# Attention scores by pairs of heads, the low keys on half of TensorE's rows

## The chip, the core and the metric

The kernel runs on one core of a Trainium2 chip. The metric is the device time of one execution in microseconds (us). Engines are named as the profile names them: PE is TensorE's matmul and PEld its weight load, DVE is VectorE, ACT ScalarE, POOL GpSimd, SP SyncE, whose queue here issues most DMAs.

## The reference

Two layers on 256 tokens of width 2048, with a context of 256 tokens: first a Fourier layer, then an attention layer with 64 query heads of 64, 8 key heads, a sink and a gate. The change lies in the second layer:

```python
def _attend_with_sink(q, k, v, sink, mask=None):
    s = jnp.einsum('bqhgd,bkhd->bhgqk', q, k).astype(jnp.float32) * (ATTN_HEAD_DIM ** -0.5)
    if mask is not None:
        s = jnp.where(mask, s, NEG_INF)
    sk = jnp.broadcast_to(sink.astype(jnp.float32)[None, :, :, None, None], s.shape[:-1] + (1,))
    p = jax.nn.softmax(jnp.concatenate([s, sk], axis=-1), axis=-1)[..., :-1]
    return jnp.einsum('bhgqk,bkhd->bqhgd', p.astype(v.dtype), v)
```

Queries come from `h @ w_in`, turned by their positions; the result is `y = o * silu(z)` with `z` from the same product, and then `x + gate * (y @ w_out)`. The keys of a query block are its band of 256 tokens and the 256 of the context: 512 keys.

## The kernel before

Numbers are carried in two parts, a high and a low one, each in float16 (weights, queries, keys, probabilities) or in a rounded float32; `mm3` makes a product out of three matmuls (L80 high by high, L81, L82 with one low part each).

The attention layer is a loop over 64 heads `i` (key head `hk = i // 8`, pair `b = i // 2`), with other matmuls of the layer as filling between its steps. `filler` emits the next unit of a list (`units`): eight `q` units make the queries of a key head, two `z` units a block of 128 gate columns, twelve `o` and six `b` units begin the output product. A unit takes 1024 columns of split weights; a split of 2048 columns is ScalarE's L180 (high part) and VectorE's L181 (low part) from a buffer `raw` that SP's queue loads, and serves two units. Six tiles `ws` hold three such splits.

The steps of one head `i`:

- `stage_s` (L1362): for each block `tb` of 128 queries two score matmuls of 512 keys. The stationary operand `qq[hk][:, i % 8, tb, :]` has the high part of a query on rows 0 to 63 and the low part on rows 64 to 127; the moving one is `kkh`, the high keys standing twice (L1373), and then `kkl`, the low keys standing twice (L1374). VectorE adds the mask and takes the maximum (L1375, followed by the read-out of that maximum), ScalarE takes the exponential with its sum (L1378) and a small one for the sink (L1379), VectorE adds the sums and inverts them (L1380, L1381). ScalarE then writes the high half of the probabilities (L1388), VectorE the low half (L1389), and SP's queue transposes both into `ft` (L1391, four buffers). The last two heads are transposed on TensorE instead (`stage_t`).
- `stage_o` (L1401): the values of a pair, 24 matmuls L1408 on 64 columns each, the two heads of the pair in the two halves of the columns. `emit_y` gates the result (L1360), once the `z` block has had its tanh (L1347, L1348).

Per head the loop calls `stage_s(i)`, one filler, at odd `i` the values of the pair that was scored before this one, and one more filler. `q_turn` (L1255) splits the queries of the next key head and transposes them; `k_turn` splits the second half of the keys, one block in each of the heads 9, 11, 13 and 15; GpSimd turns the queries (`roped`). `finish_q` puts `q_turn` off by some slots (`defer`).

PSUM has eight banks, all from one pool (`psum`); the probabilities `p` have three pairs' worth of single buffers (`bufs=3` with two tiles a head).

The order on each engine is set by a scheduler with a timeline of its own, except where `tc.issue_after(pe_last[0])` ties an instruction behind another on its engine. Before, that held for heads 0 to 3 alone (`held`).

Of the kernel before, what the change touches and what calls it, by code (L numbers as in the profile page):

```python
# [10 lines left out]
F32 = mybir.dt.float32  # L11
# [22 lines left out]
def tile_dit(ctx: ExitStack, tc: tile.TileContext, a: dict, out: bass.AP):  # L34
# [44 lines left out]
    def mm3(o, wh, wl, xh, xl, start, stop):  # L79
        PE.matmul(o, wh, xh, start=start, stop=False)  # L80
        PE.matmul(o, wh, xl, start=False, stop=False)  # L81
        return PE.matmul(o, wl, xh, start=False, stop=stop).ins  # L82
# [997 lines left out]
    with tc.tile_pool(name="h1", reuse_waits="tile", bufs=16) as h1p:  # L1080
# [76 lines left out]
        with tc.tile_pool(name="at", reuse_waits="tile", bufs=2) as at:  # L1157
# [19 lines left out]
            def o1_step(k, os_, wh, wl):  # L1177
                while len(yh) <= min(k + 4, NB - 1) and (len(yh) < 24 or fin):
                    y_split(len(yh))
                for tb in range(2):  # L1180
                    mm3(os_[tb], yh[k][:, tb * P : (tb + 1) * P], yh[k][:, N + tb * P : N + (tb + 1) * P], wh, wl, k == 0, k == NB - 1)
            def b_step(k, wh, wl):
                if k == 0:
                    oB.extend([psum() for _ in range(2)] for _ in range(2))
# [68 lines left out]
                qq[hk] = qT  # L1253

            def q_turn(tb, t, qT):  # L1255
                qf = actp.tile([P, 8, P], F16, tag="act", name="qf")
                t3 = t.rearrange("p (h d) -> p h d", d=64)
                S.copy(qf[:, :, 0:64], t3)
                V.tensor_tensor(qf[:, :, 64:128], t3, qf[:, :, 0:64], op=ALU.subtract)
                nc.sync.dma_start_transpose(qT[:, :, tb, :], qf.rearrange("p h d -> p (h d)"))  # L1260

            def units():
                order = [("q", 0)]
# [95 lines left out]
                    y1.append(act())  # L1359
                V.scalar_tensor_tensor(y1[blk // 2][:, (blk % 2) * N : (blk % 2 + 1) * N], oos.pop(blk)[:, 0:N], dscz[:, blk : blk + 1], szs.pop(blk), op0=ALU.mult, op1=ALU.mult)  # L1360

            def stage_s(i):  # L1362
                hk, blk, hh = i // 8, i // 2, i % 2
                kkh, kkl = (kk[hk // 4][:, hk % 4 * 2 + j].rearrange("p t q -> p (t q)") for j in range(2))
# [4 lines left out]
                so = []  # L1369
                for tb in range(2):  # L1370
                    o = psum()
                    st = qq[hk][:, i % 8, tb, :]
                    PE.matmul(o, st, kkh, start=True, stop=False)  # L1373
                    pe_last[0] = PE.matmul(o, st, kkl, start=False, stop=True).ins  # L1374
                    V.tensor_tensor_reduce(o, o, mask[:, tb, :], nscl[:, hk : hk + 1], nsink[:, i : i + 1], ALU.add, ALU.min, mx[:, tb : tb + 1])  # L1375
                    so.append(o)
                for tb in range(2):
                    S.activation(pt[tb], so[tb], AF.Exp, bias=mx[:, tb : tb + 1], scale=-1.0, accum_out=sm[:, tb : tb + 1])  # L1378
                S.activation(es, mx, AF.Exp, bias=sink[:, i : i + 1])  # L1379
                V.scalar_tensor_tensor(sm, sm, 1.0 / PS, es, op0=ALU.mult, op1=ALU.add)  # L1380
                V.reciprocal(sm, sm)  # L1381
                ft = at.tile([P, 8, 2, P], F16, tag="ft", name="ft", bufs=4)
                fs = []
                for tb in range(2):
                    f = act(F16, 1024)
                    if i >= 62:
                        fs.append(f)
                    S.activation(f[:, 0:512], pt[tb], AF.Copy, scale=sm[:, tb : tb + 1])  # L1388
                    V.scalar_tensor_tensor(f[:, 512:1024], pt[tb], sm[:, tb : tb + 1], f[:, 0:512], op0=ALU.mult, op1=ALU.subtract)  # L1389
# [11 lines left out]
            def stage_o(b):  # L1401
# [3 lines left out]
                for kb in range(4):  # L1405
                    for vp, fp_ in ((0, 0), (1, 0), (0, 1)):
                        for hh in range(2):
                            PE.matmul(  # L1408
                                oo[hh * 64 : hh * 64 + 64, 0:N],
                                v01[kb][:, hk, vp * 64 : vp * 64 + 64],  # L1410
                                fts[hh][:, fp_ * 4 + kb, :, :].rearrange("p t q -> p (t q)"),
# [27 lines left out]
                if defer and defer[0][0] + 2 < j:  # L1439
                    defer.pop(0)[1]()  # L1440

            def held(i):
                return tc.issue_after(pe_last[0]) if i < 4 else nullcontext()

            pts = {}
            for i in range(66):
                if 8 <= i < 16 and i % 2:
                    k_turn(1, ((i - 9) // 2,))
                if i % 8 == 0:
                    while defer:  # L1450
                        defer.pop(0)[1]()
                if i == 62:
# [3 lines left out]
                if i < 64:  # L1456
                    with held(i):
                        pts[i] = stage_s(i)
                if i - 2 >= 62:
                    stage_t(*pts[i - 2])  # L1460
                with held(i):
                    filler()
                if i >= 3 and i % 2:
                    with held(i):
                        stage_o((i - 3) // 2)
                with held(i):
                    filler()


        with tc.tile_pool(name="fin", reuse_waits="tile", bufs=1) as fp:  # L1470
# [207 lines left out]
```

## Time and profile before

| | |
|---|---|
| median of three runs | 1719.26 us (1718.33 to 1721.31) |
| the profiled execution | 1717.57 us, of which the span of its instructions is 1715.8 |
| granted TensorE clock | 0.999 |
| PE busy in the span | 1681.5 us (98%) |
| DVE, ACT, POOL busy | 1366.1 (80%), 1109.7 (65%), 250.5 us (15%) |
| scores and values (first score to last value) | 1120 to 1580 us of the span |

A row of the timeline has the start in us from the span's beginning, the length, the engine, the line, the operation, out<-in, the shapes, and in square brackets the idle time before it and what ended it. Matmuls are pipelined: the length of one (0.38 us for 512 columns) is longer than the distance to the next (0.22), and it is the distance that counts. On VectorE and ScalarE too a row's length overlaps the next one's start a little.

### The profile page before, as it was taken

What the parts mean: (1) busy time and instruction counts of PE and PEld (TensorE: products, weight loads), DVE (VectorE), ACT (ScalarE), POOL (GpSimd) and SP (SyncE); (2) the same over time, 40 slices, a digit from 0 to 9 for tenths busy, and PEclk for the clock granted to TensorE, in tenths of its full rate; (3) what the DMA queues carried; (4) which work ended last, traced back from release to release, by engine and by line L of the source; (5) the groups of instructions that cost most, each with busy time, mean ns of one, the idle gap of its engine ahead of it and who ended that gap; (6) DMA issues with size and microseconds to landing.
All of it is one profiled execution on the core that took longest, in us unless ns stands there. A gap on an engine that the chain in (4) does not pass through costs nothing.

```text
span 1715.8 us, 27525 instructions
## 1 busy us (share of the span) xinstructions
PE 1681.5 (98%) x10137; PEld 1054.2 (61%) x10137; DVE 1366.1 (80%) x2322; ACT 1109.7 (65%) x1739; POOL 250.5 (15%) x261
## 2 busy tenths in 40 slices
PE   6999999999999999999999999999999999999997
PEld 4669999744444444444444454466567655877886
DVE  5778988899878797677888666889988888886555
ACT  5445655576658577765766476777777777786443
POOL 0001212201101011010102100032102320342010
PEclk9999999999999999999999999999999999999999
DMA  9998999889988799899999989599999999977543
GB/s 392 417 354 249 288 265 279 277 294 357 337 283 306 265 342 278 273 344 326 360 365 356 342 289 401 176 241 240 250 229 238 244 248 232 239 204 265 195 174 145
DMA packets 323367, 487.06 MB, mean 284 GB/s; under 512 B 181344, under 2 KB 247280, under 8 KB 299680
## 3 DMA queue, kind: packets, MB, share of 16 engines
q1 hardware_dynamic: 299168, 447.29, 81.3%
q0 software_dynamic: 19920, 31.06, 7.2%
q10 hardware_dynamic: 4144, 6.95, 1.2%
q8 instruction: 79, 1.29, 0.3%
q14 instruction: 56, 0.46, 0.1%
HBM read 433.85 MB, written 12.59 MB: 260 GB/s over the span
## 4 chain that ended last, share of the span: by engine, by line
PE 36%; DVE 25%; DMA 16%; issue 12%; ACT 9%; SPq 1%; POOL 1%; ACTq 0%; POOLq 0%; DVEq 0%
PE ps L80 11%; PE ps L81 11%; PE ps L82 11%; DVE w L181 7%; DMA rawz<-in_adw 6%; DVE junk L758 5%; DVE ps L1375 3%; DVE act L1389 3%; ACT w L180 2%; DMA rawz<-in_wz 2%; DMA rawz<-in_wq 2%; DMA raw<-in_awp 2%; ACT act L1388 2%; DMA rawz<-in_wkv 2%; ACT sqd L162 1%
## 5 line engine op out<-in xcount | busy, mean ns | idle before, releaser
L758 DVE CUSTOM_DVE_ANT_0 junk<-rawz,cb 128x1024 bf16<-128x1024 f32 x224 | 273.6, 1221 | 61.5 <-DMA rawz<-in_adw 51.8
L81 PE MATMUL ps<-act,w 128*128 128x512 f16 x688 | 260.8, 379 | 0.0
L82 PE MATMUL ps<-act,w 128*128 128x512 f16 x688 | 258.2, 379 | 0.0
L80 PE MATMUL ps<-act,w 128*128 128x512 f16 x688 | 258.0, 379 | 0.0
L80 PEld LDWEIGHTS <-w 128*128 128x128 f16 x1536 | 150.3, 98 | 132.4 <-issue 3.0
L81 PEld LDWEIGHTS <-w 128*128 128x128 f16 x1536 | 150.3, 98 | 129.5
L82 PEld LDWEIGHTS <-w 128*128 128x128 f16 x1536 | 150.3, 98 | 128.1 <-issue 1.7
L181 DVE SCALAR_TENSOR_TENSOR w<-raw,adab,w 128x2048 f16<-128x2048 f32 x72 | 172.4, 2394 | 23.8 <-ACT w L180 23.5
L181 DVE SCALAR_TENSOR_TENSOR w<-raw,up,w 128x2048 f16<-128x2048 f32 (+1 forms) x68 | 151.1, 2223 | 37.8 <-ACT w L180 36.7
L162 ACT ACTIVATE rawz<-rawz 128x1024 f32<-128x1024 f32 x104 | 109.2, 1050 | 107.8 <-DMA rawz<-in_wq 55.5
L180 ACT ACTIVATE w<-raw,adab 128x2048 f16<-128x2048 f32 x72 | 143.4, 1992 | 29.9 <-PE ps L81 29.8
L1388 ACT ACTIVATE act<-p,sm 128x512 f16<-128x512 f32 x128 | 85.4, 714 | 87.5 <-DVE sm L1381 43.7
L80 PE MATMUL ps<-h,w 128*128 128x256 f16 x512 | 139.7, 273 | 0.0
L82 PE MATMUL ps<-h,w 128*128 128x256 f16 x512 | 139.6, 273 | 0.0
L81 PE MATMUL ps<-h,w 128*128 128x256 f16 x512 | 139.6, 273 | 0.0
L180 ACT ACTIVATE w<-raw,up 128x2048 f16<-128x2048 f32 (+1 forms) x68 | 128.5, 1891 | 16.8 <-PE ps L81 9.6
L166 POOL PARTITION_ALL_REDUCE tot<-wq x58 | 59.7, 1028 | 496.0 <-ACT sqd L162 496.0
L1389 DVE SCALAR_TENSOR_TENSOR act<-p,sm,act 128x512 f16<-128x512 f32 x128 | 100.1, 813 | 37.4 <-ACT act L1388 37.3
L80 PE MATMUL ps<-y,w 128*128 128x512 f16 x336 | 126.7, 379 | 1.2 <-ACT y L180 1.2
L81 PE MATMUL ps<-y,w 128*128 128x512 f16 x336 | 126.8, 379 | 0.0
L82 PE MATMUL ps<-y,w 128*128 128x512 f16 x336 | 126.8, 379 | 0.0
L68 DVE TENSOR_TENSOR wl<-raw,wh 128x1024 fp32r<-128x1024 f32 x61 | 78.8, 1297 | 56.2 <-ACT wh L67 55.6
(392 smaller groups left out, 3958.7 us busy)
## 6 DMA issues: line engine op xcount, KB each, us to landing
raw<-in_wz SPq DMA_DIRECT2D x64, 1024.0 KB, 5.8
rawz<-in_adw SPq DMA_DIRECT2D x128, 512.0 KB, 7.6
raw<-in_awp SPq DMA_DIRECT2D x32, 1024.0 KB, 12.7
rawz<-in_wq SPq DMA_DIRECT2D x64, 512.0 KB, 7.0
raw<-in_wo SPq DMA_DIRECT2D x64, 512.0 KB, 8.1
raw<-in_wq SPq DMA_DIRECT2D x32, 1024.0 KB, 5.6
raw<-in_wu SPq DMA_DIRECT2D x32, 1016.0 KB, 7.0
zq<-in_wz SPq DMA_DIRECT2D x40, 512.0 KB, 9.3
```

The source lines that it names most:

```text
L68: last_sub[0] = eng.tensor_tensor(l, src, h.bitcast(F32), op=ALU.subtract).ins
L80: PE.matmul(o, wh, xh, start=start, stop=False)
L81: PE.matmul(o, wh, xl, start=False, stop=False)
L82: return PE.matmul(o, wl, xh, start=False, stop=stop).ins
L162: sq_ins[0] = S.activation(dump, src, AF.Square, scale=scale, accum_out=col).ins
L166: GP.partition_all_reduce(tot, col, P, bass_isa.ReduceOp.add)
L180: last_cast[0] = S.activation(h, src, AF.Copy, scale=up).ins
L181: last_sub[0] = V.scalar_tensor_tensor(l, src, up, h, op0=ALU.mult, op1=ALU.subtract).ins
L758: V.tensor_tensor_reduce(junk, wf, cb[:, s], 1.0, 0.0, ALU.mult, ALU.add, acc[:, i, kh, fg * 2 + f, s : s + 1])
L1375: V.tensor_tensor_reduce(o, o, mask[:, tb, :], nscl[:, hk : hk + 1], nsink[:, i : i + 1], ALU.add, ALU.min, mx[:, tb : tb + 1])
L1388: S.activation(f[:, 0:512], pt[tb], AF.Copy, scale=sm[:, tb : tb + 1])
L1389: V.scalar_tensor_tensor(f[:, 512:1024], pt[tb], sm[:, tb : tb + 1], f[:, 0:512], op0=ALU.mult, op1=ALU.subtract)
```

## The change

Two heads of a pair are scored by one function, `stage_p`, which calls what is left of `stage_s` for each. In the queries the high part now stands on rows 0 to 63 for the even head of a pair and on rows 64 to 127 for the odd one (`q_turn`, in two halves). The low keys are multiplied first and by the high queries alone, with 64 rows for each head; then come the high keys on all 128 rows. The product of low queries with low keys is no longer made. Each pair does `stage_p`, four fillers, and the values of the pair before it at the end, so that they stand ahead of the next pair's scores. Every matmul of `stage_p` and `stage_o` is tied behind the last one (`tied`, line L1367 in the changed kernel), and all steps and fillers run under `held`. In the last two rounds the values stand after two and three fillers. `p` has four buffers.

```diff
-                    mm3(os_[tb], ...)
+                    pe_last[0] = mm3(os_[tb], ...)
...
             def q_turn(tb, t, qT):
-                qf = actp.tile([P, 8, P], F16, tag="act", name="qf")
-                t3 = t.rearrange("p (h d) -> p h d", d=64)
-                S.copy(qf[:, :, 0:64], t3)
-                V.tensor_tensor(qf[:, :, 64:128], t3, qf[:, :, 0:64], op=ALU.subtract)
-                nc.sync.dma_start_transpose(qT[:, :, tb, :], qf.rearrange("p h d -> p (h d)"))
+                qf = act(F16, 1024)
+                t3 = t.rearrange("p (g x d) -> p g x d", x=2, d=64)
+                q5 = qf.rearrange("p (g x b d) -> p g x b d", g=4, x=2, b=2)
+                for x in range(2):
+                    S.copy(q5[:, :, x, x, :], t3[:, :, x, :])
+                for x in range(2):
+                    V.tensor_tensor(q5[:, :, x, 1 - x, :], t3[:, :, x, :], q5[:, :, x, x, :], op=ALU.subtract)
+                nc.sync.dma_start_transpose(qT[:, :, tb, :], qf)
...
+            def stage_p(b):
+                hk = b // 4
+                kkh, kkl = (kk[hk // 4][:, hk % 4 * 2 + j].rearrange("p t q -> p (t q)") for j in range(2))
+                so = [[psum() for _ in range(2)] for _ in range(2)]
+                for tb in range(2):
+                    for x in range(2):
+                        r = slice(x * 64, x * 64 + 64)
+                        tied(so[x][tb], qq[hk][r, b % 4 * 2 + x, tb, :], kkl[r], start=True, stop=False)
+                for x in range(2):
+                    for tb in range(2):
+                        tied(so[x][tb], qq[hk][:, b % 4 * 2 + x, tb, :], kkh, start=False, stop=True)
+                for x in range(2):
+                    pts[b * 2 + x] = stage_s(b * 2 + x, so[x])
...
-                pt = [at.tile([P, 512], F32, tag="p", name="p", bufs=3) for _ in range(2)]
+                pt = [at.tile([P, 512], F32, tag="p", name="p", bufs=4) for _ in range(2)]
...
-                    o = psum()
-                    st = qq[hk][:, i % 8, tb, :]
-                    PE.matmul(o, st, kkh, start=True, stop=False)
-                    pe_last[0] = PE.matmul(o, st, kkl, start=False, stop=True).ins
...
-            def held(i):
-                return tc.issue_after(pe_last[0]) if i < 4 else nullcontext()
+            def held(b):
+                return tc.issue_after(pe_last[0])
...
-            for i in range(66):
+            for b in range(33):
...
+                if b < 32:
+                    with held(b):
+                        stage_p(b)
+                for j in range(5):
+                    if b == 32 and 0 < j < 3:
+                        stage_t(*pts[61 + j])
+                    if b and j == {31: 2, 32: 3}.get(b, 4):
+                        with held(b):
+                            stage_o(b - 1)
+                    if j < 4:
+                        with held(b):
+                            filler()
```

The lines of `stage_s` after the scores are the same, with other numbers: L1375 is L1390 in the changed kernel, L1378 L1392, L1379 L1393, L1380 and L1381 L1394 and L1395, L1388 L1402, L1389 L1403, L1360 L1363, L1347 and L1348 L1350 and L1351.

On TensorE, at a score in the second half of the stage, stood before the end of a unit, two blocks with two matmuls each into one bank, and the next unit:

```order
L82 MATMUL ps_13802<-h1_9979,w16_13725 128x256
L1373 LDWEIGHTS qT_13051
L1373 MATMUL ps_13885<-kk1_10583,qT_13051 128x512
L1374 LDWEIGHTS qT_13051
L1374 MATMUL ps_13885<-kk1_10583,qT_13051 128x512
```

Now the last matmul of the last pair's values is followed by four into four banks (the low keys), and four more into the same banks:

```order
L1367 MATMUL ps_13688<-ft_13449,v_10703 64x256
L1367 LDWEIGHTS qT_13094
L1367 MATMUL ps_13715<-kk1_10583,qT_13094 128x512
L1367 LDWEIGHTS qT_13094
L1367 MATMUL ps_13717<-kk1_10583,qT_13094 128x512
L1367 LDWEIGHTS qT_13094
L1367 MATMUL ps_13716<-kk1_10583,qT_13094 128x512
L1367 LDWEIGHTS qT_13094
L1367 MATMUL ps_13718<-kk1_10583,qT_13094 128x512
L1367 LDWEIGHTS qT_13094
L1367 MATMUL ps_13715<-kk1_10583,qT_13094 128x512
```

The banks of both heads are thus written at the start of the pair. On VectorE one head of the steady part read before (`x2` stands for both blocks):

```order
L1389 SCALAR_TENSOR_TENSOR act<-p,sm,act 128x512 x2
L1375 ISA ps,mx<-ps,mask,nsink,nscl 128x512
L1375 ISA mx 128x1
L1375 ISA ps,mx<-ps,mask,nsink,nscl 128x512
L1375 ISA mx 128x1
L181 SCALAR_TENSOR_TENSOR w_14500<-raw,adab,w_14499 128x2048
L1380 SCALAR_TENSOR_TENSOR sm<-sm,es 128x2
L1381 RECIPROCAL sm<-sm 128x2
```

And now, from the last of a pair's four L1390 (before them stand L1390 twice, L1403 and L1390):

```order
L1390 ISA ps,mx<-ps,mask,nsink,nscl 128x512
L1390 ISA mx 128x1
L1394 SCALAR_TENSOR_TENSOR sm<-sm,es 128x2
L1395 RECIPROCAL sm<-sm 128x2
L181 SCALAR_TENSOR_TENSOR w_14477<-raw,adab,w_14476 128x2048
L1394 SCALAR_TENSOR_TENSOR sm<-sm,es 128x2
L1403 SCALAR_TENSOR_TENSOR act<-p,sm,act 128x512 x2
L1395 RECIPROCAL sm<-sm 128x2
L1363 SCALAR_TENSOR_TENSOR act<-ps,adab,th 128x256
L181 SCALAR_TENSOR_TENSOR w_14524<-raw,adab,w_14523 128x2048
L1403 SCALAR_TENSOR_TENSOR act<-p,sm,act 128x512
```

The masks of both heads come first, one of the two splits stands between the two sums, and one probability is left over to the next pair. On ScalarE, in a pair of the same kind, before (one head) and now:

```order
L1378 ACTIVATE p,sm<-ps,mx 128x512 x2
L1379 ACTIVATE es<-mx,sink 128x2
L1388 ACTIVATE act<-p,sm 128x512 x2
L180 ACTIVATE w_14499<-raw,adab 128x2048
L1378 ACTIVATE p,sm<-ps,mx 128x512 x2
```

```order
L1392 ACTIVATE p,sm<-ps,mx 128x512 x2
L1393 ACTIVATE es<-mx,sink 128x2
L1392 ACTIVATE p,sm<-ps,mx 128x512
L180 ACTIVATE w_11644<-raw,adab 128x2048
L1392 ACTIVATE p,sm<-ps,mx 128x512
L1393 ACTIVATE es<-mx,sink 128x2
L1402 ACTIVATE act<-p,sm 128x512 x2
L180 ACTIVATE w_11691<-raw,adab 128x2048
L1402 ACTIVATE act<-p,sm 128x512 x2
```

The first split of a pair stands behind the third exponential, with the fourth behind it.

More of the change, by code (lines that the diff above doesn't have):

```diff
@@ L1368, in stage_s @@
                 es = at.tile([P, 2], F32, tag="es", name="es")
-                so = []
                 for tb in range(2):
-                    o = psum()
-                    st = qq[hk][:, i % 8, tb, :]
[L1373 to L1376, printed above, removed]
+                    V.tensor_tensor_reduce(so[tb], so[tb], mask[:, tb, :], nscl[:, hk : hk + 1], nsink[:, i : i + 1], ALU.add, ALU.min, mx[:, tb : tb + 1])
                 for tb in range(2):
@@ L1407, in stage_o @@
                         for hh in range(2):
-                            PE.matmul(
+                            tied(
                                 oo[hh * 64 : hh * 64 + 64, 0:N],
```

28 lines of the change are left out of this document (9 added, 19 removed).

## The prediction

> **What bounds the kernel now.** I read first the busy time of the attention stage between its ends, then its waits, then the timelines of TensorE, VectorE and ScalarE over a few heads.
>
> ```profile
> core 0: us, PE busy (x) PEld busy (x) DVE busy (x) ACT busy (x) POOL busy (x), PEclk, DMA share, GB/s
> 1150.00:1525.00 375.00, 372.11 (x2850) 250.04 (x2847) 336.69 (x562) 285.23 (x508) 85.78 (x63) 1.00 0.99 236
> ```
>
> TensorE looks like the bound (372 of 375 us at clock 1.00), but VectorE is busy for 90% too. The waits of the same stretch (who waited for whom, us in total, times, longest) tell more:
>
> ```profile
> ACT act L1388 <- issue: 41.6, 23, 3.1
> ACT act L1388 <- DVE sm L1381: 38.1, 25, 2.8
> DVE act L1389 <- ACT act L1388: 34.3, 48, 0.9
> PE ps L1408 <- DMA ft<-act: 2.9, 4, 1.1
> DVE ps L1375 <- PE ps L1374: 0.8, 1, 0.8
> ```
>
> VectorE and ScalarE wait for each other in nearly every head, and for TensorE once, 0.8 us. So those two keep a rhythm of their own. TensorE waits only for `ft`, the transposed probabilities that come out of that rhythm. The timeline of TensorE gives both paces (start, length):
>
> ```profile
> 1152.58 0.38 PE L1373 MATMUL ps<-kk,qT 128*128 128x512 f16 x1
> 1166.20 0.38 PE L1373 MATMUL ps<-kk,qT 128*128 128x512 f16 x1
> ...
> 1304.34 0.38 PE L1373 MATMUL ps<-kk,qT 128*128 128x512 f16 x1
> 1304.56 0.38 PE L1374 MATMUL ps<-kk,qT 128*128 128x512 f16 x1
> ...
> 1307.72 0.27 PE L82 MATMUL ps<-h,w 128*128 128x256 f16 x1
> 1307.92 1.50 PE L1408 MATMUL ps<-ft,v 128*64 128x256 f16 x24
> 1309.35 0.28 PE L80 MATMUL ps<-h,w 128*128 128x256 f16 x1
> ...
> 1390.80 0.30 PE L1408 MATMUL ps<-ft,v 128*64 128x256 f16 x1
> 1391.69 1.47 PE L1408 MATMUL ps<-ft,v 128*64 128x256 f16 x23 [0.59 <-DMA ft<-act]
> ...
> 1485.34 0.38 PE L1373 MATMUL ps<-kk,qT 128*128 128x512 f16 x1
> ```
>
> The first and the last row are heads 5 and 53: 332.8 us for 48 heads, 55.5 us for a key head (8 heads, 4 pairs). A pair without a wait took 13.62 us (first two rows), so TensorE's own work is 54.5 us. The difference is stalls such as the one at 1391.69. A score matmul costs 0.22 us (1304.34 to 1304.56). Now the rhythm, one head on VectorE, then on ScalarE:
>
> ```profile
> 1394.20 2.35 DVE L181 SCALAR_TENSOR_TENSOR w<-raw,adab,w 128x2048 f16<-128x2048 f32 x1
> 1396.47 0.15 DVE L1380 SCALAR_TENSOR_TENSOR sm<-sm,es 128x2 f32<-128x2 f32 x1
> 1396.66 0.17 DVE L1381 RECIPROCAL sm<-sm 128x2 f32<-128x2 f32 x1
> 1397.66 1.42 DVE L1389 SCALAR_TENSOR_TENSOR act<-p,sm,act 128x512 f16<-128x512 f32 x2 [0.46 <-ACT act L1388]
> 1398.99 0.81 DVE L1375 CUSTOM_DVE_ANT_0 ps<-ps,mask,nsink 128x512 f32<-128x512 f32 x1
> 1400.46 2.35 DVE L181 SCALAR_TENSOR_TENSOR w<-raw,adab,w 128x2048 f16<-128x2048 f32 x1
> ```
>
> ```profile
> 1396.91 1.33 ACT L1388 ACTIVATE act<-p,sm 128x512 f16<-128x512 f32 x2 [1.51 <-issue]
> 1398.15 1.99 ACT L180 ACTIVATE w<-raw,adab 128x2048 f16<-128x2048 f32 x1
> 1400.04 0.67 ACT L1378 ACTIVATE p<-ps,mx 128x512 f32<-128x512 f32 x1
> ```
>
> One turn is 6.26 us: split L181 2.27, sum and reciprocal 0.45 until ScalarE's copy L1388 starts, 0.75 until VectorE may follow, two L1389 at 0.67, two mask-and-maximum L1375 at 0.73. Other heads carry more:
>
> ```profile
> 1374.49 2.35 DVE L181 SCALAR_TENSOR_TENSOR w<-raw,adab,w 128x2048 f16<-128x2048 f32 x1
> 1409.24 0.68 DVE L1380 SCALAR_TENSOR_TENSOR sm<-sm,es 128x2 f32<-128x2 f32 x1
> 1411.24 2.27 DVE L1389 SCALAR_TENSOR_TENSOR act<-p,sm,act 128x512 f16<-128x512 f32 x2 [0.73 <-ACT act L1388]
> 1414.90 3.12 DVE L181 SCALAR_TENSOR_TENSOR w<-raw,adab,w 128x2048 f16<-128x2048 f32 x1
> 1417.95 0.41 DVE L1348 SCALAR_TENSOR_TENSOR th<-th,ps 128x256 f32<-128x256 f32 x1
> 1427.38 1.29 DVE L1259 TENSOR_TENSOR qf<-act,qf 128x512 f16<-128x512 f32 x2
> 1430.05 2.35 DVE L181 SCALAR_TENSOR_TENSOR w<-raw,adab,w 128x2048 f16<-128x2048 f32 x1
> ```
>
> ```profile
> 1405.06 1.42 POOL L1072 TENSOR_TENSOR act<-act,rope 128x512 f32<-128x512 f32 x1 [42.21 <-ACT act L1250]
> 1412.93 2.94 POOL L1078 TENSOR_TENSOR act<-act,rt 128x512 f32<-128x512 f32 x2
> ```
>
> From 1374.49 to 1430.05 are eight heads: 55.6 us, the pace of TensorE above. Once in a key head GpSimd turns the next queries (1405.06 to 1415.87); beside it VectorE's small sum takes 0.68 instead of 0.15, L1389 2.27 instead of 1.42, a split 3.12 instead of 2.35: 2.2 us and more. So VectorE with ScalarE, not TensorE, sets 55.5 us for a key head, and TensorE has 1 us of room.
>
> **The change part by part.**
>
> *Low keys on half rows.* A pair's eight score matmuls become four full ones and four on 64 rows. If two half-row matmuls run side by side, two slots of 0.22 us go: 0.43 us. The trace has no row halves; it has column halves in L1408: 24 matmuls in 1.43 us, 0.119 us for two of them, about what one full matmul of this width costs (23 from 1305.20, behind four scores, to 1307.72: 0.109). That is the nearest row and I take it; the ends are 0 saved and 0.43 saved. Not side by side, they cost what they did.
>
> The Trainium skill ("TensorE: Matmul & The Clock Gate", Part 3, Measured speedup) gives four row groups 3.07 times, not 4, so by it, as an estimate, 0.28 us for two instead of 0.22, and the saving would be 0.30 us. No run here shows row groups yet.
>
> *The place straight behind the values.* Entering L1408 took 0.20 us instead of 0.11 (1307.72 to 1307.92), and leaving it is in the 1.43 us, 0.12 over twelve times 0.109. A pair now has one more change of shape (columns, rows, full instead of columns, full): 0.12 us, bounds 0 and 0.25. TensorE's own pair falls by 0.31, a key head to 53.2 us.
>
> *Values later.* The values of a pair now stand behind eight units of projection after its scores instead of five, so `ft` has some 8 us more, and stalls like the 0.8 us at 1391.69 go. Late next is not `ft` but whatever VectorE delivers: weights and free banks.
>
> *Two heads at once, tied.* Nothing leaves VectorE or ScalarE. Their order changes. A pair without extras is now, on VectorE from its first L1375: 0.73, 0.73, a left-over of the last pair's probabilities 0.67, then the third L1375. ScalarE's third exponential follows 0.90 after that one's start (0.73 and the 0.14 of its read-out), holds it 0.66, then comes its split; VectorE's split may start 2.02 later. So far 5.71. Then VectorE's split 2.27, second sum 0.19, two probabilities 1.34, reciprocal 0.09, gating 0.39, second split 2.27, third probability 0.67: 12.9 us, of which 1.8 is VectorE waiting for ScalarE's split. Two such heads took 12.5 before. The pairs with extras, put together in the same way from the built order: in the second, the gate's L1348 (0.33) takes the last probability's place, 12.6. In the third, ScalarE's split stands behind the second small exponential, so behind the fourth L1375: VectorE's split starts at 2.86 + 0.90 + 0.20 + 2.02 = 5.98 (1.4 of it waiting); 2.27, 0.33, 0.19, 0.67, 0.09, 0.67 and 0.39 follow, 0.2 of waiting, 2.27 and 0.33: 13.4. In the fourth the query split fills the wait: four L1375 and two left-over probabilities 4.26, query 1.45, then as in the third, with a probability at the end: 13.7. In all 52.6 us. The old heads by the same rows without GpSimd's disturbance: 55.1 less 2.2, that is 52.9. So the new order is worth 0.3; more comes from the disturbance, since L1389 and the sum beside GpSimd now stand ahead of a split for which VectorE waits 1.4 us anyway. I let 1.4 of 2.2 remain: 54.0 us; bounds 52.6 and 55.0.
>
> *Query split in halves.* Four casts and four subtractions of half the width instead of two and two; two subtractions took 1.29, four halves some 1.45; it is in the 13.7. The transpose on SP's queue and its bytes stay. On that queue a pair's four transposes of probabilities now follow each other, with the two weight loads between or behind them:
>
> ```profile
> raw<-in_wz SPq DMA_DIRECT2D x64, 1024.0 KB, 5.8
> ```
>
> A load lands in 5.8 us (last column). Its buffer is free when VectorE has made the split three before it, some 17 us ahead of need in the order above, so a few us behind transposes cost nothing.
>
> *Sums, buffers.* A fourth pair of `p` buffers costs no instruction. Every pair has its own sums as before.
>
> *End.* The first `b` unit takes four banks at once, and the first of them is the one that holds the values of pair 30, which stand straight ahead of it. Their gating stands on VectorE behind the last pair's four L1375, two splits L68 and two probabilities. The rows of both:
>
> ```profile
> 1562.17 1.23 DVE L68 TENSOR_TENSOR wl<-raw,wh 128x1024 fp32r<-128x1024 f32 x1 [0.84 <-ACT wh L67]
> 1563.31 0.48 DVE L1360 SCALAR_TENSOR_TENSOR act<-ps,adab,th 128x256 f32<-128x256 f32 x1
> ```
>
> Four L1375 2.92, the second sum at 5.7 (the fourth exponential, kept back by a cast, ends there), the first probability 1.25 later, both and a split to 9.4, the gating to 9.9 us after the first L1375. TensorE gets there 8.0 us after the last scores begin (1.3, two units 5.2, values 1.5). With one to two us of lag it waits 3 us; bounds 0 and 6. Before, single matmuls of other units filled such holes.
>
> *Sum.* Key heads 2 to 6: five times 55.4 less 54.0, 7.0 us. First two: the four key turns (not changed, one in each pair of the second) fall into VectorE's wait in three pairs of four, but the lag has to build up first; I take 1.5 us. Last: TensorE's 0.31 in each of four pairs, 1.2 us. End: 3.0 lost. In all 6.7 us less. The profiled execution took 1717.6 us (span 1715.8 and 1.8 around it), 1.7 under the median of the runs; so 1712.6 against 1719.3.
>
> **Rivals.**
>
> *TensorE sets the pace after all.* If GpSimd's disturbance vanishes in VectorE's wait, VectorE needs 52.6 and TensorE 53.2. Then eight key heads win 2.2 each, less the end: 15 us, about 1705. For it: VectorE has one wait of 1.4 to 1.8 us in each pair. Against: TensorE never waited for weights, so every us there is VectorE's.
>
> *The rhythm stays.* If the disturbance is not absorbed, 55.0 us for a key head: 3 us won, the end lost, 1718 to 1719. For it: quiet pairs get 0.4 longer. Here falls also the case that two halves don't run side by side (TensorE 54.9), and DMA, at a share of 0.99 now.
>
> *New waits for banks: slower.* A pair's four scores now take the banks of the pair before it, which ScalarE's fourth exponential frees 6.3 us after VectorE's first L1375 (third exponential 3.0, then 0.66, split 1.89, 0.66), in the gate's pairs 7.6. TensorE returns after 13.3. That leaves VectorE 5.7 us of lag behind the scores. In the old order it had:
>
> ```profile
> 1373.63 0.38 PE L1373 MATMUL ps<-kk,qT 128*128 128x512 f16 x1
> ...
> 1378.96 0.81 DVE L1375 CUSTOM_DVE_ANT_0 ps<-ps,mask,nsink 128x512 f32<-128x512 f32 x1
> ```
>
> 5.3 us, from a score to its L1375. Beyond 5.7, TensorE, tied, can do nothing else until the bank is free. One us in each of 27 pairs against the gain would give some 1727, with 5 at the end. The Trainium skill ("TensorEngine Tiling (Array Packing)", Gotcha 1: PSUM Pressure) warns that row tiles need different banks; here they have them, at the price of this wait.
>
> **How the numbers follow.** Forecast (54.0) 45 in 100: 1708.5 to 1716. TensorE-bound 20: 1705. Rhythm unchanged 23: 1716 to 1721. Banks 12: 1722 to 1730. The range 1704 to 1721.5 leaves about 13 to 18 out. A measurement here tells 0.2%, 3.4 us, from no change: faster is below 1715.8. That is nearly all of the first two: 0.63; same 0.25; slower 0.12.
>
> **What the profile would show.** Right: pairs of half-row matmuls start within some 0.02 us of each other, a pair's scores take 1.3 us and not 1.73; values wait for no `ft`; a key head takes 54 us between equal scores; VectorE waits for ScalarE's split rather than for its copy. Wrong: TensorE waiting at scores for an exponential, or at projections for L181; half-row matmuls 0.22 apart; the wait at the first `b` unit over 6 us.

## The result, and the profile after

The changed kernel took 1737.95 us (median of 4 runs, 1735.65 to 1744.58); the kernel before, on the same chips, 1719.02. The ratio is 1.0114, 95% interval 1.0085 to 1.0143: **slower by about 19 us**, where 6.7 us less were forecast. The profiled execution took 1735.65 us, its span is 1733.8.

Read at three points of the two traces (first score; first score of pair 28; end), in us:

| | first score | from it to pair 28 | pair 28 to the end |
|---|---|---|---|
| before | 1120.1 | 386.6 | 209.0 |
| changed | 1122.9 | 399.1 | 211.8 |

The first column is scatter: ahead of the first score TensorE's order is the same in all kernels here (only the split of the first queries differs, by the halves), and the first score came between 1118.7 and 1124.2. Of the 18.1 us between the two profiled executions 12.5 arise up to pair 28 (the steady part), 2.8 behind it, and 2.8 are this scatter. The steady part's busy time between the ends of the stretch shown of before:

```profile
1150.00:1525.00 375.00, 356.17 (x2770) 235.44 (x2769) 327.39 (x564) 274.70 (x490) 65.85 (x48) 0.99 1.03 234
```

All engines do less in the same time (TensorE 356 of 375 us instead of 372), so none became the bound by work of its own. The waits of the stretch:

```profile
DVE w L181 <- ACT w L180: 24.7, 19, 1.8
DVE act L1363 <- PE ps L1367: 19.5, 17, 4.1
PE ps L1367 <- DMA ft<-act: 18.8, 14, 3.1
ACT w L180 <- PE ps L81: 6.6, 9, 1.3
```

TensorE waits for `ft` 18.8 us instead of 2.9, and VectorE, which before never waited for a pair's values, now does so 17 times when it gates them (L1363): each waits for the other, in a loop that is called the chain below. One turn of it, first on TensorE:

```profile
1346.58 0.30 PE L1367 MATMUL ps<-ft,v 128*64 128x256 f16 x1
1348.60 1.50 PE L1367 MATMUL ps<-ft,v 128*64 128x256 f16 x23 [1.72 <-DMA ft<-act]
...
1361.96 1.50 PE L1367 MATMUL ps<-ft,v 128*64 128x256 f16 x24
1363.39 1.57 PE L1367 MATMUL ps<-kk,qT 64*128 64x512 f16 x8
1364.80 0.27 PE L80 MATMUL ps<-h,w 128*128 128x256 f16 x1
```

then on VectorE, behind those values, and on SP's queue:

```profile
1350.14 0.48 DVE L1363 SCALAR_TENSOR_TENSOR act<-ps,adab,th 128x256 f32<-128x256 f32 x1 [2.35 <-PE ps L1367]
1350.54 2.34 DVE L181 SCALAR_TENSOR_TENSOR w<-raw,adab,w 128x2048 f16<-128x2048 f32 x1
1353.46 0.81 DVE L1390 CUSTOM_DVE_ANT_0 ps<-ps,mask,nsink 128x512 f32<-128x512 f32 x1
1354.92 0.75 DVE L1403 SCALAR_TENSOR_TENSOR act<-p,sm,act 128x512 f16<-128x512 f32 x1
1356.32 0.81 DVE L1390 CUSTOM_DVE_ANT_0 ps<-ps,mask,nsink 128x512 f32<-128x512 f32 x1
```

```profile
1352.91 0.33 SPq L51 DMA_DIRECT2D raw<-in_wq  x1
1353.61 4.74 SPq L1405 DMA_TRANSPOSE ft<-act  x2
```

The values of pair 14 wait for `ft`; their gating waits for them; the split behind the gating ends at 1352.9 and frees a `raw` buffer; SP's queue sets off the 1 MB load of the next weights at once (1352.91), and right behind it the last two transposes of pair 15 (1353.61 and 1355.7). These land at 1359.6 and 1361.9, and the values of pair 15 start at 1361.96. From values to values that is 15.4 us; TensorE's own pair is 13.4. A wait can cost more than its length: behind the waits of 2.8 and 3.1 us that ended at 1177.24 and 1405.89 the granted TensorE clock was 0.50 for 3.4 us, and the 23 value matmuls took 2.77 us instead of 1.47. That is some 2.6 of the 12.5 us. How long a transpose took, before and after (count, median us from issue to landing in 1150 to 1500):

```profile
ft<-act SPq DMA_TRANSPOSE x101, 4.4
```

```profile
ft<-act SPq DMA_TRANSPOSE x99, 5.9
```

The same two traces show what the longer time consists of. Of about 100 transposes in each, over 90 were issued while a load was under way, and none of those landed before that load; the first behind a load landed 1.0 us after it by the median. When a transpose was issued, the load ahead had on average 2.7 us left before the change and 3.8 now, and that is most of the difference between the mean times of the transposes (4.6 and 5.7). Only 2 transposes were issued within 1 us of a load before; now it is 23, and they took 6.6 us.

The budget of `ft`, as means over pairs 8 to 26, in us: from a pair's first score to VectorE's first mask (the lag), from there to the end of its last probability, from there to the landing of its transpose, the sum, and the earliest that its values started in any of these pairs, which is their place by TensorE's order alone. The experiments below are in the same table.

| | score to mask | mask to last probability | to landing | sum | values' place |
|---|---|---|---|---|---|
| before | 4.3 | 13.8 | 4.8 | 22.9 | 23.2 |
| changed | 3.5 | 17.1 | 5.9 | 26.5 | 25.2 |
| probabilities first (e5) | 4.9 | 14.5 | 7.7 | 27.1 | 25.2 |
| no weight loads (e9) | 4.0 | 16.4 | 3.4 | 23.8 | 25.2 |
| both (e10) | 6.8 | 13.7 | 4.1 | 24.6 | 25.2 |
| values a pair later (e1) | 6.1 | 9.9 | 6.5 | 22.5 | 31.0 |
| straight behind scores (e7) | 5.8 | 9.8 | 6.5 | 22.2 | 28.4 |

Where the sum stays under the last column, TensorE hardly waits. In the changed kernel and in e5 it is over it.

### The profile page after: what moved, and what is told of

It reads as the page before. It is cut to its first block, busy times and chain, and to the rows that moved or that the text cites. A ratio compares the mean times of both kernels' runs of the same rounds, so it can differ in the third digit from the quotient of the medians.

```text
span 1733.8 us, 27558 instructions
## 1 busy us (share of the span) xinstructions
PE 1677.1 (97%) x10137; PEld 1050.1 (61%) x10137; DVE 1362.9 (79%) x2338; ACT 1110.6 (64%) x1755; POOL 239.6 (14%) x261
## 5 line engine op out<-in xcount | busy, mean ns | idle before, releaser
L181 DVE SCALAR_TENSOR_TENSOR w<-raw,adab,w 128x2048 f16<-128x2048 f32 x72 | 174.4, 2423 | 50.0 <-ACT w L180 49.8
L181 DVE SCALAR_TENSOR_TENSOR w<-raw,up,w 128x2048 f16<-128x2048 f32 (+1 forms) x68 | 151.0, 2222 | 36.4 <-ACT w L180 35.2
L180 ACT ACTIVATE w<-raw,adab 128x2048 f16<-128x2048 f32 x72 | 143.7, 1996 | 38.6 <-PE ps L81 37.1
L1392 ACT ACTIVATE p<-ps,mx 128x512 f32<-128x512 f32 x128 | 86.8, 682 | 84.3 <-DVE mx L1390 84.0
L180 ACT ACTIVATE w<-raw,up 128x2048 f16<-128x2048 f32 (+1 forms) x68 | 128.4, 1890 | 10.3 <-DVE up L171 6.6
L81 PE MATMUL ps<-w,h 128*128 128x512 f16 x320 | 121.3, 379 | 0.0
```

The costliest lines, as they stand in the source:

```text
L180: last_cast[0] = S.activation(h, src, AF.Copy, scale=up).ins
L181: last_sub[0] = V.scalar_tensor_tensor(l, src, up, h, op0=ALU.mult, op1=ALU.subtract).ins
```

## The experiments

Ratios are to the kernel before on the same chip, with their 95% intervals. The edits are shown in short; comments and pointed brackets stand for parts left out.

**e1: values a pair later.** The softmax is cut in two (`stage_s` to the reciprocal, `stage_f` with `ft`), so that four `ft` do:

```diff
-                    if b and j == {31: 2, 32: 3}.get(b, 4): stage_o(b - 1)
+                    if 1 < b and j == 1: stage_o(b - 2)
+                    if b < 32 and j == 1: pts[...] = stage_f(...)   # both heads of b
+                    if b == 32 and j == 3: stage_o(b - 1)
```

> The changed kernel, but the values of a pair stand a whole pair and one unit later: behind the scores and one filler of the next but one pair, and its four transposes are written down behind them, so that four buffers ft still do. Theory (closed chain): the changed kernel's pace is one chain around the engines, from a pair's values on TensorE to their gating on VectorE, the split behind it, the next pair's four masks with the last two probabilities between them, their transposes, and so to the next values; 14 to 15 us for a pair where TensorE alone needs 13.4. With the values a pair later the chain is open: TensorE's waits for ft (18.8 us) and VectorE's for the values (20.3 us) go nearly all, a pair takes 13.4 to 13.8 us, and the time falls from 1738 to 1713 to 1722. Rival (VectorE and ScalarE need 14.2 us for a pair in two-head order whatever TensorE does): 1733 to 1740, the wait only moves to splits or scores.

1714.16 us, ratio 0.9986 (0.9976 to 0.9996). TensorE's waits for `ft` and VectorE's for values are gone from the list; key heads 2 and 3 take 53.9 us each, and 2 to 6 take 54.3 on average. So the chain through `ft` was the loss. The edit also changes VectorE's order (all four probabilities of a pair now stand in its own pair), so it does not tell which part of the chain counts.

**e2: gating later**, for pairs 0 to 23 (except where a pair's `z` block ends after its values).

```diff
-                emit_y(b)                     # end of stage_o
+                if b > 23: emit_y(b)
...
+                    if j == 1 and 1 < b < 26: emit_y(b - 2)
```

> The changed kernel with the gating of pairs 0 to 23 written down one filler into the next pair instead of directly behind the values; nothing else differs. Closed chain: the link from values to the split is gone; what is left, scores to masks, probabilities, transposes, values, is some 13 us, so VectorE's waits for values nearly vanish and most of the 0.9 us a pair above 13.4 goes: 1720 to 1728. Rival (VectorE's own order is the pace): 1733 to 1740.

1737.17 us, 1.0104 (1.008 to 1.0128): no gain. TensorE still waits 17.4 us for `ft`. The gating was mostly a symptom: VectorE's waits for values fell from 20.3 to 8.9 us, but it is held by other things that wait for TensorE (ScalarE's splits L180 waited 24.1 us for buffers instead of 15.0).

**e3: full rows.**

```diff
-                        tied(so[x][tb], qq[hk][r, b % 4 * 2 + x, tb, :], kkl[r], start=True, stop=False)
+                        tied(so[x][tb], qq[hk][:, b % 4 * 2 + x, tb, :], kkl, start=True, stop=False)
```

> The changed kernel with the low keys on all 128 rows again (a pair's first four score matmuls are then one behind the other; low queries times low keys is added, as before the change). The rows alone are undone. By the closed chain TensorE has room in every second pair: a pair's scores grow from 1.4 to 1.7 to 1.8 us, the time by 0 to 4 us: 1736 to 1742. Rival (TensorE's own work and its stalls add up): 0.4 us in each of 32 pairs, 1750.

1740.29 us, 1.013 (1.0112 to 1.0148), about 2 us more than the changed kernel, with intervals that overlap. A pair without a wait took 13.68 us instead of 13.36: the half rows save 0.32 us on TensorE, and of the 10 us that this makes in 32 pairs only some 2 reach the time; the rest goes into waiting.

**e4: half rows in the kernel before.** The rows go by block of queries instead of by head; the order is that of before.

```diff
-                    PE.matmul(o, st, kkh, start=True, stop=False)
-                    PE.matmul(o, st, kkl, start=False, stop=True)
+                    r = slice(64 * tb, 64 * tb + 64)        # first for both tb
+                    PE.matmul(os2[tb], qq[hk][r, i % 8, tb, :], kkl[r], start=True, stop=False)
+                    PE.matmul(os2[tb], qq[hk][:, i % 8, tb, :], kkh, start=False, stop=True)
```

> The kernel before with half rows alone: the high queries stand on the lower rows for the first block of queries and on the upper for the second, and each head's two low-key matmuls come first, side by side, then its two full ones, tied. Order by heads, place of the values and gating as before. If VectorE with ScalarE set the pace before (55.1 of 55.5 us for a key head), 0.2 us less on TensorE per head gives nothing but the stalls: 1715 to 1720. Rival (TensorE sets it): 64 times 0.2, 1706 to 1708.

1720.63 us, 1.0016 (1.0005 to 1.0027). That is 0.6 us above the range expected if VectorE sets the pace, but it says nothing for that: the half rows saved nothing on TensorE. One head's scores, with the last unit matmul ahead and the first behind:

```profile
1372.58 0.27 PE L82 MATMUL ps<-h,w 128*128 128x256 f16 x1
1372.78 0.39 PE L1376 MATMUL ps<-kk,qT 64*128 64x512 f16 x2
1373.11 0.60 PE L1379 MATMUL ps<-kk,qT 128*128 128x512 f16 x2
1373.55 0.27 PE L80 MATMUL ps<-h,w 128*128 128x256 f16 x1
```

From 1372.58 to 1373.55 are 0.97 us; before, the same stretch (1367.42 to 1368.39) also took 0.97. The slot saved (0.216) went into entering half rows (0.205 instead of 0.109 behind the last unit) and leaving them (0.319 instead of 0.216). Since TensorE's pace did not change, this run does not tell whether VectorE bounds the kernel before.

**e5: probabilities first.** VectorE's order changes (and, by the scheduler, the places of some of ScalarE's exponentials and splits); TensorE's doesn't.

```diff
+                    with tc.issue_after(<last L1403 of the pair before>):
                         V.tensor_tensor_reduce(so[tb], so[tb], mask[:, tb, :], ...)
```

> The changed kernel with one thing moved: on VectorE the last two low probabilities of a pair stand ahead of the next pair's four masks instead of between and behind them (the masks are tied behind them). TensorE's order, the place of the values and of the gating are as in the changed kernel. Theory (the transposes miss the values' place because the probabilities stand behind the next masks): ft lands some 3 us sooner, TensorE's waits for ft nearly go, a key head takes 53.5 to 55 us instead of 57: 1714 to 1722. Rival (the values' place itself is too early, or transposes behind weight loads are the cause): waits halve at best, 1728 to 1738.

1743.4 us, 1.0144 (1.013 to 1.0158): no gain; this theory fell, and the time lies above the rival's range too. The table shows why: the last probability was ready 1.2 us sooner after the scores (19.4 instead of 20.6), but its transpose took 1.8 us longer to land, since the transposes now stand closer behind a load (37 of 97 were issued within 1 us of one). Its transposes (same view):

```profile
ft<-act SPq DMA_TRANSPOSE x98, 6.1
```

**e9 and e10: no weight loads.** In the attention stage all q and z splits read one `raw` buffer loaded once; e9 is otherwise the changed kernel, e10 is e5.

```diff
-                    raws1[src] = raw(...)
+                    raws1[src] = keep[0] if keep else raw(...)
```

> The changed kernel without the loads of the q and z weights in the attention stage (from the third key head's queries on, all splits read one buffer that was loaded once; the products are those of wrong weights). The order on TensorE, VectorE and ScalarE is the same, instruction by instruction. In the changed kernel a transpose of probabilities took 5.7 us from issue to landing on average, 6.1 where a weight load of 1 MB ran beside it most of the time and 3.8 where hardly any did; before the change 4.6. Theory (the transposes collide with the loads that the splits ahead of them set off): ft lands about 2 us sooner, the waits for ft fall from 18.8 us to under 6, time 1718 to 1728. Rival (VectorE's order alone, the load only changes who waits): 1731 to 1738.

> The fifth experiment (all probabilities of a pair ahead of the next pair's masks) without the weight loads, as in the ninth. There the last probability was ready 1.5 us sooner after the scores, but its transposes, three behind each other and a load between, took 1.8 us longer. If both matter, the loads' part comes back here and the gain is larger than in the ninth: 1712 to 1722. If VectorE's own pair in that order (13.9 us, 1.9 of it waiting for ScalarE's split) is the pace, 1730 to 1738.

e9 took 1713.2 us, 0.9964 (0.995 to 0.9978), the whole 25 us less and below the expected range, with the order on TensorE, VectorE, ScalarE and GpSimd unchanged. The loads did not act by another way: in the changed kernel no split waited for one, and the instructions of VectorE and ScalarE took as long with the loads as without (L181 2.44 us on average in both, the exponential 0.68). Its transposes, and what is left of the wait (same columns as above):

```profile
ft<-act SPq DMA_TRANSPOSE x105, 3.2
```

```profile
PE ps L1369 <- DMA ft<-act: 2.2, 4, 1.0
```

So in this order the collision of the transposes with the loads is what closes the chain; without it the order of the changed kernel runs at 53.9 us for a key head. e10 took 1717.58 us, 0.9992 (0.9983 to 1.0001), as expected, but not better than e9: VectorE's waits for ScalarE's splits (6.1 us in a key head, as in e5, where e9 has 4.5) make its own order 54.4 us for a key head. Once the transposes are fast, it doesn't matter that two probabilities stand behind the next masks.

**e8: untied.**

```diff
-                with tc.issue_after(pe_last[0]):                # tied
-                    pe_last[0] = PE.matmul(*args, **kw).ins
+                pe_last[0] = PE.matmul(*args, **kw).ins
...
-                return tc.issue_after(pe_last[0])               # held
+                return tc.issue_after(pe_last[0]) if b < 2 else nullcontext()
```

> The changed kernel without the ties behind pair 1: neither scores and values nor fillers are held in the order written, so the scheduler may put other matmuls between (in every other pair it puts the first value matmul ahead of four scores, and in some of them breaks up the half rows' row). If the ties are what makes TensorE stand at the values, its waits for ft fall by half or more: 1718 to 1728. If the late probabilities are the cause, little changes: 1732 to 1740.

1726.1 us, 1.0042 (1.0028 to 1.0056). By the median 12 us come from untying, but in the profiled run key heads 2 to 6 still took 57.8 us on average (57.1 with the ties), and TensorE still waited 13.8 us for `ft` (less by a quarter, not by half); the gain was in the first key head (51.0 us instead of 57.0) and in the end (208.5 us behind pair 28 instead of 211.8). So the ties cost time at both ends, but the loss of the steady part isn't theirs.

**e6 and e7: towards a version that gains.** e6 is e1 with the first line below, e7 is e6 with the second.

```diff
-                    if j not in ready and (j == pos[0] + 1 or ulist[j][0] in "qz"):
+                    if j not in ready and (j == pos[0] + 1 or ulist[j][0] in "qzo"):
...
-                    if 1 < b and j == 1: stage_o(b - 2)
+                    if 1 < b and j == 0: stage_o(b - 2)
```

> The first experiment (values a pair later) with one more change at its end: the splits of the first output product's units are made two units ahead instead of one, as those of q and z are. There TensorE stood some 8 us, first for ScalarE's cast of such a split (3.1 us), then for VectorE's part, then at half its clock. If that cast was only made too late, most of the 8 us goes: 1705 to 1710. If ScalarE had no room for it, 1711 to 1716.

> As the last one, but the values of the pair before last stand straight behind a pair's scores, without a filler between, so half rows, full rows and columns follow each other and one change of shape goes. In the steady part each pair has 0.1 us less if a change of shape costs 0.1 us (3 us in all) as far as VectorE (53 to 54 us for a key head) lets it: 1702 to 1709; rival: the gating or banks now make TensorE wait, 1710 to 1716.

e6: 1715.05 us, 0.9983 (0.9973 to 0.9994); the early splits brought nothing. e7: 1713.62 us, 0.9976 (0.9966 to 0.9986), faster than both kernels, yet short of what was expected: its steady part is 10.7 us shorter than before the change, but behind pair 28 it takes 216.8 us instead of 209.0.

**e11, e12: the end untied (without and with the early splits). e13, e14: back to one pair behind at pair 27**, the end tied and untied.

```diff
+                    ... tied and held only for b < 28            # e11, e12, e14
-                    if 1 < b and j == 0: stage_o(b - 2)
+                    if 1 < b <= 27 and j == 0: stage_o(b - 2)    # e13, e14
+                    if b >= 27 and j == {31: 2, 32: 3}.get(b, 4): stage_o(b - 1)
```

> The version towards which the runs point: the values of the pair before last straight behind a pair's scores (as in the seventh, without its earlier splits), all tied up to pair 27, and from pair 28 on nothing tied, so that the scheduler may fill TensorE's waits at the end. In the seventh, from pair 28's scores to the end 216.8 us passed, in the untied eighth 208.5. Expected: 376 us for 28 pairs as in the seventh and 208 to 211 behind: 1705 to 1710. Rival (the filled holes only move, since ScalarE's casts are the limit there): 1711 to 1716.

> The eleventh with the splits of the output product's units two units ahead, as in the seventh. In the sixth this was worth nothing against the first (21.3 instead of 21.6 us for the slow round). Expected: within 2 us of the eleventh; rival: with free matmuls to fill the waits the earlier splits pay, 3 to 5 us below it.

> The version of the seventh experiment (scores, then the values of the pair before last; no early splits), but from pair 27 on the values stand one pair behind again and where the changed kernel has them; all tied. If what is lost behind pair 28 comes from values being two pairs late at the end (the last gatings, splits of the output product's inputs), the part behind pair 28 falls from 217 to 211 or 212 us, as in the changed kernel, with 376 us ahead of it: 1708 to 1712. Rival (ScalarE's casts are late there in any order): 1713 to 1717.

> The thirteenth with nothing tied from pair 28 on, as in the eighth experiment, where the part behind pair 28 took 208.5 us, and in the kernel before, where it took 209.1. Expected 376 plus 208 to 210: 1705 to 1709. Rival: as the eleventh showed for values two pairs behind, the free matmuls gain nothing, 1710 to 1715.

e11 1715.4 us (0.9982, 0.9972 to 0.9992) and e13 1716.15 (0.9988, 0.9978 to 0.9998) miss what was expected and lie in the ranges of their rivals; e12 1715.92 (0.9977, 0.9967 to 0.9987) is within 2 us of e11, as expected. e14, 1712.1 us, **0.9967 (0.9955 to 0.9979)**, has the lowest ratio of the kernels that leave nothing out, though the intervals of e7 and e15 overlap its own, and its time is in the rival's range; behind pair 28 it takes 213.0 us, not the 208 to 210 expected.

**e15: e7 with full rows**, the edit of e3.

> The seventh experiment with the low keys on all 128 rows again. There TensorE set the pace, 53.9 us for a key head, VectorE needed 54.9. A pair has two slots of 0.216 us more and one change of shape less (0.1 us): 55.1 to 55.2 us for a key head, 5 to 9 us more in all: 1719 to 1723. Rival (VectorE's 54.9 is the real pace, the rest is absorbed): 2 to 4 us more, 1715 to 1718.

1713.89 us, 0.9977 (0.9968 to 0.9986): the same as e7, against both expectations. Its steady part is indeed 4.8 us longer (54.73 us for a key head, TensorE's own, instead of 53.9), but behind pair 28 it takes 211.1 us instead of 216.8. Where the two meet again is VectorE's first mask of pair 28, e15 first, then e7:

```profile
1502.36 0.81 DVE L1390 CUSTOM_DVE_ANT_0 ps<-ps,mask,nsink 128x512 f32<-128x512 f32 x1
```

```profile
1504.62 0.81 DVE L1390 CUSTOM_DVE_ANT_0 ps<-ps,mask,nsink 128x512 f32<-128x512 f32 x1
```

The first scores were at 1119.34 and 1121.73, so VectorE needed 383.0 and 382.9 us to that mask, the same. In e7 TensorE's score of pair 28 was 6.9 us ahead of that mask, in e15 2.3 us. What TensorE gains over VectorE's pace (54.9 us for a key head in both) only becomes lead, and the end takes it back. So with the chain open VectorE with ScalarE is the bound, and the half rows are worth nothing measurable.

**e16: the kernel before without the loads**, the edit of e9.

> The kernel before without the loads of q and z weights in the attention stage, as in the ninth (wrong weights). If VectorE with ScalarE set its pace, as predicted (55.1 us for a key head), the steady part keeps 55 us and only the waits for ft (4 us) can go: 1713 to 1719. Rival (the loads set it there too): 54.7 us, TensorE's own, and the end faster as well, 1706 to 1712.

1715.85 us, 0.999 (0.9979 to 1.0001): its transposes took 3.2 us as well, but by the interval it gained 4 us at most; VectorE's first masks were 55.0 us apart for a key head (pairs 12 to 24; 55.4 with the loads). So the same loads cost the old order a few us at most and the changed one 25.

## Why the prediction was wrong

- **The step that failed: "ft has some 8 us more, and stalls like the 0.8 us at 1391.69 go".** Counted from the pair's first score, at which both heads now begin, the values' place moved from 23.2 to 25.2 us, 2 us and not 8. The 8 us hold for the second head alone, and its probabilities moved too: the working for VectorE already had the left-over probabilities between and behind the next pair's masks, which by its own terms is some 15 to 18 us behind a pair's first mask (measured 17.1, before 13.8), and the sum of lag, this time and a transpose was never set against the place of the values. With the transpose of before, 4.8 us, it would have been 25.4 against 25.2: no slack. It was 26.5, so TensorE waited 18.8 us for `ft` and not 0.
- **"A few us behind transposes cost nothing"** looked at one side of the queue. The load may be late; the transposes behind it may not. VectorE's split frees the buffer that starts the load, and in the new order the transposes come right behind it: 5.9 us instead of 4.4 by the median. Of the two terms that grew, the later probability is the larger (3.3 us against 1.1), but moving it alone gained nothing (e5), since the transposes then took longer still, and taking away the loads alone gained everything (e9). The profile before gave a hint of it, a DMA share of 0.99.
- **TensorE's own part was right.** Forecast 0.31 us less for a pair and 53.2 us for a key head; measured 0.32 (e3) and 53.4 (the forecast took the shortest pair of before, 13.62 us, for all four; they took 54.7 us together and not 54.5). The half-row matmuls of a pair start 0.003 us apart, the scores take 1.41 us instead of 1.73. The estimate of 0.28 us for two half rows, worked out from what the Trainium skill ("TensorE: Matmul & The Clock Gate", Part 3, Measured speedup) gives for four row groups, is not borne out for two: the second couple starts 0.22 us behind the first.
- **VectorE's working came out in size**: 54.0 us forecast, 53.9 in e9, where hardly anything waits for `ft` or values. Some of that is luck: the waits for ScalarE's split were put at 1.4 to 1.8 us in every pair and were 1.8, 1.8, 0.6 and 0.3, and TensorE's own 53.4 lies close by. In the changed kernel itself it is 57.1, since it waits for values.
- **That VectorE with ScalarE, not TensorE, set the pace before** is supported, not proven: e16 keeps 55.0 (TensorE's own is 54.7), and e15 against e7 shows the same bound in another order. **The rival "rhythm stays"** had the DMA share in it, as a case of no change; that was the place where "slower" belonged.
- **The rival that named the right sign, waits for banks, did not happen**: no score waited for an exponential. The time put on it, 1727, does not come out of its own terms either: 1719.3 less the 9.7 us of gain, plus 27 and 5, is some 1742. So "slower" had its chance of 0.12 for a reason that did not occur.
- **The end: the size near by luck, the wait not right.** Forecast 3.0 us lost less 1.2 won, so 1.8 more behind pair 28; measured 2.8 more. No wait at the first `b` unit shows; TensorE stood at an `o` unit, for ScalarE's cast of a gated result:

```profile
1560.73 0.50 PE L80 MATMUL ps<-wh,act 128*128 128x512 f32 x1 [3.40 <-ACT act L67]
```

- Key heads 2 to 6 were forecast at 7.0 us less and took 8.4 more (285.5 us against 277.1); the first two 1.5 less, 4.1 more (113.6 against 109.5).

Open: whether the transposes waited for their turn behind the load on the one queue, as the order of landing suggests, or shared the DMA engines with it; e9 takes away both, and no run put the loads on another queue. Why the end takes 206 to 212 us from VectorE's first mask of pair 28 in every version was not tried further.

## What to carry to other kernels

When a consumer is moved later, write down its deadline and the whole way to it in the new order (lag, the producer's queue, the transfer) from one and the same starting point, and compare sums. Ask of every buffer that an instruction frees which transfer it sets off, and what else is on the DMA engines then: a transfer of 4.4 us became one of 5.9 when it came to be issued closer behind a load. A gain on an engine that is not the bound showed up as lead here, and was given back where the lead ended (e15 against e7).

## What the runs showed of the hardware

- A change between full, half-row and half-column shapes costs TensorE 0.10 us each (0.205 instead of 0.109 us entering, 0.308 instead of 0.216 leaving half rows; columns to half rows, 0.205, is one change). So two half-row matmuls between full ones save nothing (e4), and four behind the values save 0.32 us. The Trainium skill ("TensorEngine Tiling (Array Packing)", Key Properties) says that changing the tiling mode drains TensorE; the runs show a cost at each change, which agrees, and give its size.
- A transpose of 256 KB took 3.2 us by the median without loads (e9, e16). With loads of 1 MB on the same queue it depended on how closely it followed one: in the changed kernel 6.6 us on average when issued within 1 us of a load, 5.6 from 2 to 4 us behind it, 3.7 from 6 us on. None landed before a load that was under way when it was issued.
- Behind some waits of about 3 us TensorE ran at half its clock for 3.4 us more: in the changed kernel, behind the wait of 3.40 us that ended at 1560.73, the granted clock was 0.50 from 1562.3 to 1565.7, and matmuls were 0.43 us apart instead of 0.23 (1563.55 to 1563.98 below), which costs another 1.5 us. The Trainium skill ("TensorE: Matmul & The Clock Gate", Part 1) has the clock halved behind an idle window of about 3.4 us that runs freely; the length of the stretch agrees, but two waits of only 2.8 and 3.1 us in the changed kernel were followed by one too, and waits of 3.4 us in e9 and e13 were not.

```profile
1563.55 0.63 PE L81 MATMUL ps<-wl,act 128*128 128x512 f32 x1
1563.98 1.05 PE L82 MATMUL ps<-wh,act 128*128 128x512 f32 x2
```
